# One layer of a streaming encoder: low parts of output-projection weights, two plain up-projection pairs and token sums by accumulating DMAs, and the second norm's squares and rows in more buffers

## The chip, the cores and the metric

The kernel runs on one core of a Trainium2 chip. The metric is the device time of one execution in microseconds. Before the change three runs took 1517.62, 1519.51 and 1512.99 us, a median of 1517.62.

## What is computed

A block with 16 meta tokens ahead of 1024 tokens of width 1024: a norm, then attention and a state-space model beside each other, merged by gates and projected by `w_o`; a second norm, then a gated convolutional feed-forward layer; a final norm. All in float32.

```python
def _mixer(xn, w_in, b_forget, w_attn_out, ..., w_glu, w_o):
    ...
    y_a = _forgetting_attention(q, k, v, f_logit, b_forget) @ w_attn_out
    ...
    merged = g[..., :D_MODEL] * y_a + g[..., D_MODEL:] * y_s
    return merged.astype(xn.dtype) @ w_o

def _conv_ffn(xn, w_up, conv_w, conv_b, w_down):
    hid = xn @ w_up
    hp = jnp.pad(hid, ((0, 0), (CONV_WIDTH - 1, 0), (0, 0)))
    conv = conv_b + sum(hp[:, j:j + seq_len] * conv_w[j] for j in range(CONV_WIDTH))
    val, gate = jnp.split(conv, 2, axis=-1)
    return (jax.nn.silu(gate) * val) @ w_down

def reference(x, meta_tokens, ...):
    h = jnp.concatenate([meta, x], axis=1)
    xn = _rmsnorm(h, norm_mix_g)
    h = h + _mixer(xn, ...)
    xn = _rmsnorm(h, norm_ffn_g)
    h = h + _conv_ffn(xn, w_ffn_up, ffn_conv_w, ffn_conv_b, w_ffn_down)
    return _rmsnorm(h, norm_final_g)[:, N_META:]
```

## The kernel before

**Split operands.** Every float32 matrix is kept as two tiles in a shorter matmul format: `hi`, a copy of it rounded by the copy, and `lo`, what the rounding left over. A product then takes three matmuls: hi by hi, hi by lo, lo by hi. For each operand tile somebody makes `hi` (mostly ScalarE, L940, L1113, L260; for the attention's output weights GpSimd, L149) and then `lo = source - hi`, which is `split_lo` (L128, recorded as L129) on VectorE or GpSimd. One older helper makes `lo` otherwise: `lo_by_dma` (L133) has ScalarE write minus `hi` (L135), and then a DMA issued by GpSimd adds the source from DRAM to it (L136). Before the change it serves early weights alone (`w_g`, `w_q`, `w_k`).

**Order.** The program is written as plain loops; a scheduler fixes the order of each engine's instructions when the kernel is built, and at run time each engine works through its own list in that order. DMAs stand in the list of the engine that issues them: SP (SyncE) issues the plain loads, POOL (GpSimd) the accumulating ones, and a DMA whose inputs aren't ready holds what is behind it in that list. Tiles come from pools with a set number of buffers for each tag; a tile waits until the buffer's last readers are done.

**The merge** (L948 to L963, 668.5 to 719.5 us of the span). For each of 8 row blocks `i`, `wchunk(w_ao[i], 4)` loads 128x512 weights into `raw` and makes `whi` and `wlo` (two buffers each in the pool `wp`); 36 matmuls (L958 to L960) form the attention's output, VectorE multiplies by the gate (L961) and adds into `merged[i]` (tile `mr`, L962). Beside that, `out_forms` makes the operands of products 0 and 4 of the next stage in the memory of `xhi` and `xlo`.

**The output products** (719.5 to 811.1 us). `merged` by `w_o` is done with seven products of half-size blocks (`out_product`, in the order 0, 4, 1, 5, 2, 3, 6), each with 4 blocks of tokens and 48 matmuls (L1015 to L1017). Products 1, 2, 3 and 5 use sums of weight blocks formed earlier in DRAM (`to_d`). `operands(p)` loads the weights of later products (`out_weights`, tile `wr`) and has `out_forms` make operands of the left (from `mr`) and the right (from `wr`). Of its low parts those of products 0, 4 and 5 are GpSimd's and the others VectorE's. Rows of `h2` are finished by VectorE (L1021) and, for product 2, GpSimd (L1024).

**The second norm** (`normed`, from product 6 on). For each of 9 blocks of rows: ScalarE sums the squares (L170), VectorE and GpSimd make the factor (L172, L174), VectorE scales into `xs` (L179), TensorE transposes (L187), ScalarE writes `xhi` and VectorE `xlo` (L189, L129). The squares go to the same `xs` tile, of which there are two.

**The up projection** (from 811.1 us). Pairs of gate and value columns: pair 0 and pair 1 are plain (`plain_pair`: weights in four `sw` tiles for each half, matmuls L1165 to L1167, then the convolution's taps on ScalarE L1169 and VectorE L1171, tiles `og` and `ov`). `xn_forms` makes sums of token halves for the other pairs: for each of four `k`, `fa` and `fb` by GpSimd (L1185) and VectorE (L254 to L258), then hi and lo (`t0h`, `t0l` to `t3l`). `fa` and `fb` share three buffers of the tag `h`, which later pairs use too. Pairs 2 to 20 use seven half-size products (`block_pair`, `seven`), with sums of weights by GpSimd (`sf`, L1121); the last pair, 21, is plain again. GpSimd also issues accumulating DMAs of the down projection's weight sums (L1139) from pair 2 on.

Of the kernel before, what the change touches and what calls it, by code (L numbers as in the profile page):

```python
# [9 lines left out]
F = mybir.dt.float32  # L10
# [9 lines left out]
P = 128  # L20
# [30 lines left out]
def block_kernel(ctx, tc, x, meta, g1, x0t, g1t, w_q, w_k, w_v, w_f, w_u, w_g, b_f, w_ao, lam_d, bw_d, cw_d,  # L51
# [86 lines left out]
    def wchunk(src, k, eng=None, act=False):  # L138
        raw = wp.tile([P, k, P], F, tag="raw", name="raw", padded_shape=[P, KD, P])
        ld = (GP if act else SY).dma_start(raw, src)  # L140
        if act:
            after(ld, late[0])
        hi = wp.tile([P, k, P], R, tag="whi", name="whi", padded_shape=[P, KD, P])
        lo = wp.tile([P, k, P], R, tag="wlo", name="wlo", padded_shape=[P, KD, P])
        if act:
            S.copy(hi, raw)
            lo_by_dma(lo, hi, src)
            return hi, lo
        GP.tensor_scalar(hi, raw, 1.0, 0.0, ALU.mult, ALU.add)  # L149
        split_lo(eng or V, lo, raw, hi)  # L150
        return hi, lo
# [25 lines left out]
    def norm_rows(pl, src, n, gB, xs):  # L177
        rs = norm_factor(pl, src, n, 3, xs)
        V.scalar_tensor_tensor(out=xs[:n], in0=src, scalar=rs[:n], in1=gB[:n], op0=ALU.mult, op1=ALU.mult)  # L179
# [67 lines left out]

    def token_forms(k, whole, f, T):
# [10 lines left out]
        for f_, t_ in zip((f3, f2, f1, f4), (T[2], T[1], T[0], T[3])):  # L259
            S.copy(t_[0], f_)  # L260
            split_lo(V, t_[1], f_, t_[0])
# [626 lines left out]
    merged = [mp.tile([P, LQ], F, name=f"mr{i}") for i in range(KD)]  # L888
# [30 lines left out]
    def out_weights(p, q, pl, tag, bufs=2):  # L919
# [4 lines left out]
        wr[p, 2 * q], wr[p, 2 * q + 1] = t_[:, 0], t_[:, 1]  # L924

    def out_forms(p, j):
# [12 lines left out]
        for q, src in ((0, (a11, a11, a11, a21, a12, a22, a11)[p]), (2, wr.pop((p, j)))):  # L939
            S.copy(slot[q], src)  # L940
            split_lo(GP if p in (0, 4, 5) else V, slot[q + 1], src, slot[q])
# [6 lines left out]
    for i in range(KD):  # L948
# [5 lines left out]
        whi, wlo = wchunk(w_ao[i], 4)  # L954
# [70 lines left out]

    def normed(c, dst, n):
        xs = n2.tile([P, D], F, tag="xs", name="xs", bufs=2)
        norm_rows(n2, dst, n, g2B, xs)
        to_feature(xs, n, xhi, xlo, TILES[c][0] if c else T0)
        if c:  # L1030
            SY.dma_start(h_d[P * (c - 1):P * c], dst)
# [3 lines left out]
    tags = {1: "raw", 5: "whi", 2: "wlo", 3: "raw", 6: "whi"}  # L1035
# [114 lines left out]
    def plain_pair(c, parts=(QBLK,)):  # L1150
        res = []
        ws = {}
        for part, (m, tag) in ((part, mt) for part in parts for mt in ((NFF + c, "og"), (c, "ov"))):
            if m not in ws:
                raw = up_raw(m)
                ws[m] = [split_q(raw[:, KH * q:KH * q + KH]) for q in range(2)]
# [629 lines left out]
```

## Time and profile before

| | before |
|---|---|
| runs, us | 1517.62, 1519.51, 1512.99 |
| profiled execution, its own time | 1517.67 us |
| its span, first to last instruction | 1515.9 us |
| mean granted TensorE clock | 0.983 |
| instructions | 26588 |
| merge | 668.5 to 719.5 us |
| output products | 719.5 to 811.1 us |
| end of product 6 to the start of pair 2 | 811.1 to 882.1 us |

The profile is of one execution. PE is TensorE's matmuls, PEld its weight loads, DVE VectorE, ACT ScalarE, POOL GpSimd, SP SyncE. A row of waits reads: the engine and line that waited, what ended the wait, total us, times, the longest. A row of groups reads: line, engine, operation, output from inputs, shapes, count, then busy us and the mean ns of one, then the idle time ahead of it and what ended that. In a table of windows PEclk is the TensorE clock granted, 1 being full speed, and the DMA share is that of all 16 engines. "Landing" is the time from the issue of a DMA to its end. In the page's rows L numbers are lines of the kernel before.

### The profile page before, as it was taken

Reading aid. Unit: us, or ns where it says so; the run is one execution under the profiler, and the core shown is the slowest. Engines: PE = TensorE matmul, PEld = TensorE weight load, DVE = VectorE, ACT = ScalarE, POOL = GpSimd, SP = SyncE. Lnnn points to the kernel's source line nnn. Section 1 sums busy time; section 2 is a strip of 40 time slices with the busy share of each in tenths; the row PEclk is TensorE's granted clock in tenths of the full one; section 3 lists DMA queues with packets and bytes.
Section 4 is the critical chain, followed back from the end, with each engine's and each line's share of the span. In section 5 each row is a group of like instructions: output and inputs, shape, how many; then the busy total and the mean of one; then the engine's idle time right before and its main releaser. Section 6 shows DMA issues by size and latency. Waiting matters only on the chain.

```text
span 1515.9 us, 26588 instructions
## 1 busy us (share of the span) xinstructions
PE 1447.7 (96%) x9736; PEld 1363.6 (90%) x9736; DVE 1093.1 (72%) x2178; ACT 697.6 (46%) x1351; POOL 782.2 (52%) x866
## 2 busy tenths in 40 slices
PE   7999997999999999999998799999999999999997
PEld 6989997998999999998787799999999999878886
DVE  7878748871656676645777987888887774798785
ACT  6334665531546565540435444444444444444343
POOL 1411136760546555546852645555544326599766
PEclk9999999999999999999999899999999999999999
DMA  6365572551027422164533146676643214774413
GB/s 241 94 163 141 141 139 63 164 168 51 23 78 192 128 55 92 43 251 152 211 88 135 43 105 174 174 189 180 166 114 98 73 68 167 290 238 127 138 49 111
DMA packets 88150, 201.46 MB, mean 133 GB/s; under 512 B 14330, under 2 KB 25210, under 8 KB 87636
## 3 DMA queue, kind: packets, MB, share of 16 engines
q1 hardware_dynamic: 69956, 161.83, 32.7%
q0 software_dynamic: 11840, 27.28, 10.1%
q10 hardware_dynamic: 6224, 10.65, 1.9%
q8 instruction: 77, 1.26, 0.3%
q14 instruction: 53, 0.43, 0.1%
HBM read 160.65 MB, written 69.35 MB: 152 GB/s over the span
## 4 chain that ended last, share of the span: by engine, by line
PE 78%; DVE 9%; DMA 6%; issue 3%; POOL 2%; ACT 2%; SPq 0%; POOLq 0%; DVEq 0%; ACTq 0%
PE mm L155 4%; PE mm L157 4%; PE mm L156 4%; PE sp L215 4%; PE sp L216 4%; PE sp L217 4%; PE mm L215 3%; PE tp L215 3%; PE mm L217 3%; PE tp L216 3%; PE mm L216 3%; PE tp L217 3%; PE tp L752 2%; PE po L774 1%; PE po L773 1%
## 5 line engine op out<-in xcount | busy, mean ns | idle before, releaser
L155 PE MATMUL mm<-xhi,whi 128*128 128x342 f32 (+2 forms) x488 | 159.4, 327 | 1.0 <-DVE q L129 1.0
L157 PE MATMUL mm<-xhi,wlo 128*128 128x342 f32 (+2 forms) x488 | 158.3, 325 | 0.0
L156 PE MATMUL mm<-xlo,whi 128*128 128x342 f32 (+2 forms) x488 | 157.7, 324 | 0.0
L1144 POOL TENSOR_TENSOR ov<-ov,og 128x1024 f32<-128x1024 f32 x21 | 51.3, 2441 | 130.7 <-ACT og L1143 127.9
L129 DVE TENSOR_TENSOR sw<-sf,sw 128x512 fp32r<-128x512 f32 x76 | 70.7, 931 | 52.5 <-ACT sw L1113 52.5
L1113 ACT CAST sw<-sf 128x512 fp32r<-128x512 f32 x76 | 47.5, 625 | 112.1 <-POOL sf L1121 79.2
L155 PEld LDWEIGHTS mm<-xhi,whi 128*128 128x128 f32 x488 | 91.9, 188 | 2.1 <-PE sp L710 0.8
L157 PEld LDWEIGHTS mm<-xhi,wlo 128*128 128x128 f32 x488 | 91.8, 188 | 0.3
L156 PEld LDWEIGHTS mm<-xlo,whi 128*128 128x128 f32 x488 | 91.9, 188 | 0.2
L217 PE MATMUL mm<-xhi,sw 128*128 128x256 f32 (+1 forms) x304 | 85.5, 281 | 0.0
L215 PE MATMUL mm<-xhi,sw 128*128 128x256 f32 (+1 forms) x304 | 85.3, 281 | 0.0
L216 PE MATMUL mm<-xlo,sw 128*128 128x256 f32 (+1 forms) x304 | 85.2, 280 | 0.0
L759 ACT CAST th<-tp 128x256 fp32r<-128x256 f32 (+3 forms) x120 | 56.2, 472 | 61.8 <-PE tp L752 28.1
L129 DVE TENSOR_TENSOR tl<-tp,th 128x256 fp32r<-128x256 f32 (+3 forms) x120 | 65.2, 547 | 25.8 <-ACT th L759 24.4
L724 POOL TENSOR_SCALAR pt<-pt,nm 128x144 f32<-128x144 f32 (+4 forms) x72 | 51.6, 729 | 50.7 <-DVE nm L723 49.7
L1121 POOL TENSOR_TENSOR sf<-raw,sf 128x512 f32<-128x512 f32 x38 | 62.2, 1638 | 27.4 <-DVE sw L129 27.4
L1206 DVE SCALAR_TENSOR_TENSOR ov<-hv,cwt,ov 128x1024 f32<-128x1024 f32 x38 | 74.2, 1953 | 0.2
L1121 POOL TENSOR_TENSOR sf<-raw 128x512 f32<-128x512 f32 x38 | 49.9, 1314 | 45.9 <-DVE sw L129 21.7
L1113 ACT CAST sw<-raw 128x512 fp32r<-128x512 f32 x69 | 42.4, 620 | 58.9 <-PE sp L217 27.8
L722 ACT ACTIVATE pt<-pt,nm 128x144 f32<-128x144 f32 (+4 forms) x72 | 52.9, 735 | 27.3 <-DVE nm L721 26.9
L715 DVE CUSTOM_DVE_ANT_0 pt<-sp,fb 128x328 f32<-128x328 f32 (+8 forms) x112 | 46.4, 430 | 19.5 <-PE sp L710 11.3
L129 DVE TENSOR_TENSOR sw<-raw,sw 128x512 fp32r<-128x512 f32 x69 | 57.6, 842 | 3.5 <-ACT sw L1113 2.6
(693 smaller groups left out, 5733.9 us busy)
## 6 DMA issues: line engine op xcount, KB each, us to landing
raw<-in_w_up_dram SPq DMA_DIRECT2D x44, 512.0 KB, 3.7
t_d<-in_w_dn_dram POOLq DMA_DIRECT2D x44, 256.0 KB, 6.9
ar<-a_d SPq DMA_DIRECT2D x44, 256.0 KB, 4.9
wr<-t_d SPq DMA_DIRECT2D x44, 256.0 KB, 2.9
a_d<-ov SPq DMA_DIRECT2D x21, 512.0 KB, 2.6
wr<-in_w_dn_dram SPq DMA_DIRECT2D x33, 256.0 KB, 3.4
t_d<-in_w_dn_dram SPq DMA_DIRECT2D x22, 256.0 KB, 4.7
t_d<-t_d SPq DMA_DIRECT2D x22, 256.0 KB, 4.7
```

The lines of the kernel that those rows point to most:

```text
L129: return eng.tensor_tensor(out_, src, hi.bitcast(F), ALU.subtract)
L155: yield PE.matmul(ps, whi[:, i, :], ahi[:, i], start=(i == 0), stop=False)
L156: yield PE.matmul(ps, whi[:, i, :], alo[:, i], start=False, stop=False)
L157: yield PE.matmul(ps, wlo[:, i, :], ahi[:, i], start=False, stop=(i == k - 1))
L215: PE.matmul(ps, a[0][:, i], bh, start=(i == 0 and not joins), stop=False, skip_group_check=True)
L216: PE.matmul(ps, a[0][:, i], bl, start=False, stop=False, skip_group_check=True)
L217: PE.matmul(ps, a[1][:, i], bh, start=False, stop=(i == kh - 1), skip_group_check=True)
L722: S.activation(pt[:n, :kc], pt[:n, :kc], AF.Exp, bias=nm[:n, 1:2], scale=0.125, accum_out=nm[:n, 2:3])
L759: S.copy(th[:kn, z:tw], tp[:kn, z:tw])
L1113: S.copy(hi, src)
L1121: sums.append(GP.tensor_tensor(f_, a, b, op))
L1206: V.scalar_tensor_tensor(out=o, in0=h_[:, j:SEQ + j], scalar=cwc(j, m), in1=o, op0=ALU.mult, op1=ALU.add)
```

## The change

Four edits. First, `wchunk` gets a switch `dma`, on for the eight chunks of `w_ao`: `hi` by a ScalarE copy, `lo` by `lo_by_dma`. Second, `out_forms` makes the low parts of all 28 right-hand tiles by `lo_by_dma`, from `w_o` or `to_d`; the left-hand ones stay. Third, a new `neg_lo` (VectorE writes minus `hi`, a DMA of POOL adds the source) takes the place of `split_lo` in `token_forms` (16 tiles, source the SBUF tiles `fa` and `fb`) and in `plain_pair` (12 tiles, source `w_up` in DRAM). Fourth, the second norm's squares go to a bf16 tile of their own in the `wlo` buffers of `wp`, and its rows `xs` to two buffers of `n2`, the two `whi` buffers of `wp`, the buffer of `mr0`, and, for the meta rows, in place; the `wr` tiles of product 6 move from `whi` to `wlo`. That is 8 + 28 + 16 + 12 = 64 accumulating DMAs more on POOL.

```diff
--- before.py
+++ after.py
@@ -135,14 +135,14 @@
         S.activation(lo, hi.bitcast(F), AF.Copy, scale=-1.0)
         GP.dma_start(lo, src.bitcast(R), accum_op=ALU.add)
 
-    def wchunk(src, k, eng=None, act=False):
+    def wchunk(src, k, eng=None, act=False, dma=False):
         raw = wp.tile([P, k, P], F, tag="raw", name="raw", padded_shape=[P, KD, P])
         ld = (GP if act else SY).dma_start(raw, src)
         if act:
             after(ld, late[0])
         hi = wp.tile([P, k, P], R, tag="whi", name="whi", padded_shape=[P, KD, P])
         lo = wp.tile([P, k, P], R, tag="wlo", name="wlo", padded_shape=[P, KD, P])
-        if act:
+        if act or dma:
             S.copy(hi, raw)
             lo_by_dma(lo, hi, src)
             return hi, lo
@@ -174,8 +174,8 @@
         GP.tensor_tensor(rs[:n], va[:n], nhalf[:n], ALU.pow)
         return rs
 
-    def norm_rows(pl, src, n, gB, xs):
-        rs = norm_factor(pl, src, n, 3, xs)
+    def norm_rows(pl, src, n, gB, xs, sq=None):
+        rs = norm_factor(pl, src, n, 3, sq)
         V.scalar_tensor_tensor(out=xs[:n], in0=src, scalar=rs[:n], in1=gB[:n], op0=ALU.mult, op1=ALU.mult)
 
     def to_feature(xs, n, dhi, dlo, col, bank=st_ps):
@@ -245,6 +245,10 @@
         S1, A22, S4 = split_q(s1), split_q(a22), split_q(s4)
         return [A11, S3, S2, S1, A12, A22, S4]
 
+    def neg_lo(lo, hi, src):
+        V.tensor_scalar(lo, hi.bitcast(F), -1.0, None, ALU.mult)
+        GP.dma_start(lo, src.bitcast(R), accum_op=ALU.add)
+
     def token_forms(k, whole, f, T):
 
         f1, f2, f3, f4 = f
@@ -258,7 +262,7 @@
         V.tensor_tensor(f4, f4, f2, ALU.subtract)
         for f_, t_ in zip((f3, f2, f1, f4), (T[2], T[1], T[0], T[3])):
             S.copy(t_[0], f_)
-            split_lo(V, t_[1], f_, t_[0])
+            neg_lo(t_[1], t_[0], f_)
 
     turn = [0]
 
@@ -885,7 +889,7 @@
     mm_n[1] = True
     st_o = ExitStack()
     mp = pool(st_o, "merged", side="right")
-    merged = [mp.tile([P, LQ], F, name=f"mr{i}") for i in range(KD)]
+    merged = [mp.tile([P, LQ], F, tag=f"mr{i}", name=f"mr{i}") for i in range(KD)]
 
     st_m = ExitStack()
     mg = pool(st_m, "mergein", side="left")
@@ -921,7 +925,8 @@
         t_ = pl.tile([P, 2, 512], F, tag=tag, name="wr", bufs=bufs)
         src = (o_block(*own_w[p]) if p in own_w else to_d[p])[256 * q:256 * q + 256]
         SY.dma_start(t_, src.rearrange("(c p) d -> p c d", p=P))
-        wr[p, 2 * q], wr[p, 2 * q + 1] = t_[:, 0], t_[:, 1]
+        for i in range(2):
+            wr[p, 2 * q + i] = t_[:, i], src[P * i:P * i + P]
 
     def out_forms(p, j):
 
@@ -936,9 +941,12 @@
         elif p == 6:
             GP.tensor_tensor(a11, a11, a12, sub)
         slot = slots_of[p][j]
-        for q, src in ((0, (a11, a11, a11, a21, a12, a22, a11)[p]), (2, wr.pop((p, j)))):
-            S.copy(slot[q], src)
-            split_lo(GP if p in (0, 4, 5) else V, slot[q + 1], src, slot[q])
+        a_ = (a11, a11, a11, a21, a12, a22, a11)[p]
+        S.copy(slot[0], a_)
+        split_lo(GP if p in (0, 4, 5) else V, slot[1], a_, slot[0])
+        b_, src = wr.pop((p, j))
+        S.copy(slot[2], b_)
+        lo_by_dma(slot[3], slot[2], src)
 
     ga0 = side_loads(0)
     for mm in gate_chunk(KD - 1, mg, True):
@@ -951,7 +959,7 @@
         mi = merged[i]
         if i % 2 == 0:
             out_weights((0, 4)[i // 4], i % 4 // 2, mg, "wr", 4)
-        whi, wlo = wchunk(w_ao[i], 4)
+        whi, wlo = wchunk(w_ao[i], 4, dma=True)
         for t, n in QBLK:
             ps = mm_ps()
             for m, oh, ol in os_:
@@ -1023,16 +1031,23 @@
             for d_, op in ((bot[:, l_], ALU.add), (bot[:, r_], ALU.subtract), (top[:, r_], ALU.subtract)):
                 GP.tensor_tensor(d_, d_, u2[t], op)
 
+    rows = {c: (n2, "xs", 2) for c in (5, 6, 2, 3)} | {c: (wp, "whi", 2) for c in (7, 8, 4)} | {1: (mp, "mr0", 1)}
+
     def normed(c, dst, n):
-        xs = n2.tile([P, D], F, tag="xs", name="xs", bufs=2)
-        norm_rows(n2, dst, n, g2B, xs)
+        if c:
+            pl, tag, bufs = rows[c]
+            xs = pl.tile([P, D], F, tag=tag, name="xs", bufs=bufs)
+        else:
+            xs = dst
+        sq = wp.tile([P, 2 * D], BF, tag="wlo", name="sq")
+        norm_rows(n2, dst, n, g2B, xs, sq[:, :D])
         to_feature(xs, n, xhi, xlo, TILES[c][0] if c else T0)
         if c:
             SY.dma_start(h_d[P * (c - 1):P * c], dst)
 
 
     after_of = {None: (1,), 0: (5,), 4: (2,), 5: (3, 6)}
-    tags = {1: "raw", 5: "whi", 2: "wlo", 3: "raw", 6: "whi"}
+    tags = {1: "raw", 5: "whi", 2: "wlo", 3: "raw", 6: "wlo"}
 
     def operands(p):
         for nx in after_of.get(p, ()):
@@ -1153,7 +1168,13 @@
         for part, (m, tag) in ((part, mt) for part in parts for mt in ((NFF + c, "og"), (c, "ov"))):
             if m not in ws:
                 raw = up_raw(m)
-                ws[m] = [split_q(raw[:, KH * q:KH * q + KH]) for q in range(2)]
+                ws[m] = []
+                for q in range(2):
+                    ks = slice(KH * q, KH * q + KH)
+                    hi, lo = ring()
+                    S.copy(hi, raw[:, ks])
+                    neg_lo(lo, hi, w_up[m][:, ks])
+                    ws[m].append((hi, lo))
                 res.append(conv_out(m, tag))
             w2, o = ws[m], res[len(ws) - 1 if len(ws) < 2 else int(m == c)]
             for t, n in part:
```

The edits shift later line numbers: L931 to L937 become L936 to L942, L1121 becomes L1136, L1144 L1159, L1165 to L1167 L1186 to L1188, L1171 L1192, L1185 L1206, and L254 to L258 of the token sums L258 to L262. The DMAs of `neg_lo` are L250, its negations L249.

**POOL in the merge.** The first chunks' weights, the sigmoid's last step (`gs`), the left (`mr`) and right (`wr`, `w_o`) operands of product 0. Before:

```order
L149 TENSOR_SCALAR whi<-raw 128x512
L442 TENSOR_SCALAR gs<-gs 128x1026
L129 TENSOR_TENSOR xhi<-wr,xhi 128x512 x4
L149 TENSOR_SCALAR whi<-raw 128x512
L129 TENSOR_TENSOR xhi<-mr_8508,xhi 128x512
L129 TENSOR_TENSOR xlo<-wr,xlo 128x512
L931 TENSOR_TENSOR mr_8508<-mr_8508 128x512
```

And now, in the same place:

```order
L446 TENSOR_SCALAR gs<-gs 128x1026
L136 DMA wlo<-in_w_ao_dram 128x512
L136 DMA xhi<-in_w_o_dram 128x512 x4
L136 DMA wlo<-in_w_ao_dram 128x512
L129 TENSOR_TENSOR xhi<-mr_8508,xhi 128x512
L136 DMA xlo<-in_w_o_dram 128x512
L936 TENSOR_TENSOR mr_8508<-mr_8508 128x512
```

The second chunk's high part is gone from POOL, and the transfer of its low part stands behind `gs`; the third chunk's stands behind four transfers of product 0.

**POOL behind the second norm.** The last factors of the norm, then the token sums. Before, no DMA stands there:

```order
L174 TENSOR_TENSOR rs<-vr,nhalf 128x1 x4
L1185 TENSOR_TENSOR fa<-xhi,xlo 128x514
L1185 TENSOR_TENSOR fb<-xhi,xlo 128x514
L1185 TENSOR_TENSOR fa<-xhi,xlo 128x514 x3
L1185 TENSOR_TENSOR fb<-xhi,xlo 128x514 x2
L1185 TENSOR_TENSOR fa<-xhi,xlo 128x514 x2
```

And now:

```order
L174 TENSOR_TENSOR rs<-vr,nhalf 128x1 x4
L1206 TENSOR_TENSOR fa<-xhi,xlo 128x514
L1206 TENSOR_TENSOR fb<-xhi,xlo 128x514
L1206 TENSOR_TENSOR fa<-xhi,xlo 128x514 x3
L250 DMA sw<-in_w_up_dram 128x512 x5
L1206 TENSOR_TENSOR fb<-xhi,xlo 128x514
L250 DMA sw<-in_w_up_dram 128x512
L250 DMA t2l<-fb 128x514
L250 DMA sw<-in_w_up_dram 128x512 x2
L250 DMA t0l<-fa 128x514
```

The low parts of pair 0's weights (`sw`) come behind five token sums, and the later token sums behind those transfers.

**TensorE at the end of the second norm.** The last transposes (L187) and pair 0. Before, matmuls of pair 0 stand between them:

```order
L187 MATMUL sp<-ident,xs 128x128 x4
L187 MATMUL tp<-ident,xs 128x128 x4
L1167 MATMUL po<-xhi,sw 128x256
L1165 MATMUL po<-xhi,sw 128x256
L1166 MATMUL po<-xlo,sw 128x256
L1167 MATMUL po<-xhi,sw 128x256
```

And now:

```order
L187 MATMUL sp<-ident,xs 128x128 x4
L187 MATMUL tp<-ident,xs 128x128 x4
L1186 MATMUL mm<-xhi,sw 128x258
L1187 MATMUL mm<-xlo,sw 128x258
L1186 MATMUL mm<-xhi,sw 128x256
L1187 MATMUL mm<-xlo,sw 128x256
```

All transposes of the norm now come first, and pair 0 begins with the matmuls by its weights' high part.

## The prediction, made before the change was run

> **What bounds the kernel now.** First the page's busy line and its chain of work by engine.
>
> ```profile
> span 1515.9 us, 26588 instructions
> PE 1447.7 (96%) x9736; PEld 1363.6 (90%) x9736; DVE 1093.1 (72%) x2178; ACT 697.6 (46%) x1351; POOL 782.2 (52%) x866
> PE 78%; DVE 9%; DMA 6%; issue 3%; POOL 2%; ACT 2%; SPq 0%; POOLq 0%; DVEq 0%; ACTq 0%
> ```
>
> TensorE works 96% of the span. No matmul is removed, so only its gaps, and time at a low clock, can change. All 64 new transfers lie where the table by stage puts the merge (first row), the output products (second), and the norm with pairs 0 and 1 (third); the fourth is the first ordinary pair, the fifth and sixth lie around one stall.
>
> ```profile
> core 0: us, PE busy (x) PEld busy (x) DVE busy (x) ACT busy (x) POOL busy (x), PEclk, DMA share, GB/s
> 668.50:719.50 51.00, 47.41 (x290) 46.69 (x289) 28.59 (x38) 10.22 (x17) 36.87 (x36) 0.97 0.63 221
> 719.50:811.10 91.60, 88.83 (x398) 71.31 (x397) 71.02 (x81) 38.02 (x69) 58.38 (x48) 0.98 0.49 174
> 811.10:882.10 71.00, 57.26 (x385) 56.11 (x384) 62.59 (x85) 33.88 (x62) 35.73 (x27) 0.86 0.16 45
> 882.10:902.10 20.00, 20.00 (x171) 20.00 (x169) 15.52 (x24) 7.95 (x15) 11.30 (x8) 1.00 0.42 123
> 685.00:690.00 5.00, 1.57 (x10) 1.28 (x9) 1.64 (x4) 0.00 (x0) 5.00 (x6) 0.94 0.21 82
> 690.00:695.00 5.00, 5.00 (x24) 4.85 (x25) 4.15 (x4) 0.62 (x1) 3.11 (x4) 0.72 0.37 95
> ```
>
> TensorE's waits between 655 and 900 us, by what ended them:
>
> ```profile
> PE mm L1165 <- DVE og L1171: 11.2, 2, 8.5
> PE mm L958 <- POOL whi L149: 3.4, 1, 3.4
> PE sp L1015 <- DVE h L1021: 2.8, 1, 2.8
> PE sp L187 <- DVE xs L179: 2.6, 1, 2.6
> ```
>
> The merge loses 3.4 us to POOL and (1 - 0.72) x 5 = 1.4 us of clock behind it; the products lose 2.8. The third stage loses most. A matmul of 256 to 258 columns takes 20.00/171 = 0.117 us at full clock. Pair 0 has 192 of these, 22.5 us; pair 1 has 144 of 342 to 344 columns, and at 0.117 x 343/257 = 0.156 us they need 22.5; the 48 transposes need about 5. That is 50 of 71 us: **21 us** are lost there, 13.7 idle and the rest at low clock. The chain between 811 and 885 us says to whom:
>
> ```profile
> by line: issue 9.1%; PE mm L1165 9.1%; PE mm L1166 8.7%; PE mm L1167 8.1%; DVE fa L255 6.0%; DVE sw L129 5.7%; DVE fa L257 5.4%; DVE t2l L129 5.3%; DVE t1l L129 3.9%; PE sp L187 3.7%; DVE og L1171 3.7%; DVE fb L254 3.2%; ACT xhi L189 2.9%;
> 833.98 4.98 issue
> 870.46 1.46 DVE og L1171 x3
> ```
>
> VectorE's sums and subtractions (L254 to L258, L129) hold the `og` steps that free pair 1's banks.
>
> **Part A: the eight w_ao chunks.** Rows of POOL, VectorE and ScalarE; the older accumulating transfers (L136, with their times to landing), and queue 0 from 900 to 1100 us:
>
> ```profile
> 668.79 0.62 POOL L149 TENSOR_SCALAR whi<-raw 128x512 fp32r<-128x512 f32 x1 [13.06 <-PE po L156]
> 669.94 1.68 POOL L442 TENSOR_SCALAR gs<-gs 128x1026 f32<-128x1026 f32 x1 [0.53 <-ACT gs L436]
> 672.49 6.26 POOL L129 TENSOR_TENSOR xhi<-wr,xhi 128x512 fp32r<-128x512 f32 x4 [0.87 <-ACT xhi L940]
> L129 DVE TENSOR_TENSOR wlo<-raw,whi 128x512 fp32r<-128x512 f32 x7 | 7.6, 1088 | 5.2 <-POOL whi L149 5.1
> L940 ACT CAST xhi<-mr 128x512 fp32r<-128x512 f32 x12 | 7.4, 620 | 23.9 <-DVE mr L962 17.0 <-PE tp L1016 6.7
> L136 POOL DMA_DIRECT2D wlo<-in_w_g_dram x7: 862/872/1222, 73.1 to 171.4; - x7
> DMA to landing us min/median/max: 6.3/7.3/13.1
> q0 software_dynamic: 5184, 9.44, 29.1%
> L1139 POOL DMA_DIRECT2D t_d<-in_w_dn_dram x44: 796/1122/1758, 873.8 to 1158.7; - x44
> DMA to landing us min/median/max: 3.7/5.7/8.9
> t_d<-in_w_dn_dram POOLq DMA_DIRECT2D x44, 256.0 KB, 6.9
> ```
>
> Removed: eight POOL copies of 0.62 us, eight VectorE subtractions of 1.09, the 3.4 us wait and its 1.4 of clock: **-5**. Added for a chunk: two ScalarE passes (0.62 each, the negation taken like the cast) and one POOL issue of 0.87. An accumulating 512 KB lands after 6.3 to 13.1 us. Queue 0 moved 9.44 MB in 29.1% of 200 us, 58.2 us; 36 pieces of 256 KB, **1.6 us** each. One 256 KB lands between 3.7 and 8.9 (L1139's landing row, which mixes POOL and SP issues; POOL's own have a median of 6.9 where they queue behind one another). A 512 KB piece less 1.6 us of traffic is 4.7 at its least and 5.7 at its median; I take **5** for a piece with none ahead.
>
> The second chunk's transfer stands on POOL behind L442, whose end is 671.6; issued at 672.5 it lands at 677.5, and the first chunk's matmuls end about 674.5. Some of the next chunk's `whi` matmuls are pulled ahead, so I count 2 to 3 us. The third stands behind the four `xhi` transfers, which share the queue with loads: four pieces at 1.6 put it 4.5 us late. The fourth costs about 3. Later chunks turn two buffers round in 0.62 + 0.62 + 5 = 6.2 us where a chunk's 36 matmuls take 36 x 0.156 = 5.6 and some have been waited for: at most 1 us a chunk, and clock of about 2. Costs together +8, so A is **+3**. If transfers land in 3.7 all waits but one go (-4); at 8.9 each of the first three waits grows by 2 (+9).
>
> **Part B: 28 right-hand tiles.** Of these 12 came from POOL and 16 from VectorE:
>
> ```profile
> L129 POOL TENSOR_TENSOR xhi<-wr,xhi 128x512 fp32r<-128x512 f32 x8 | 11.7, 1496 | 3.1 <-PE tp L995 2.2 <-ACT xhi L940 0.9
> L129 DVE TENSOR_TENSOR op<-wr,op 128x512 fp32r<-128x512 f32 x8 | 7.5, 934 | 0.0
> L129 DVE TENSOR_TENSOR xlo<-wr,xlo 128x512 fp32r<-128x512 f32 x4 | 6.9, 1772 | 0.0
> 755.00:760.00 5.00, 3.15 (x9) 2.55 (x10) 4.19 (x6) 1.14 (x2) 1.91 (x2) 0.77 0.08 21
> ```
>
> POOL gives up 1.50 us a tile and gets 0.87; VectorE gives up 0.93 to 1.77 a tile; ScalarE gets 28 x 0.62 = 17.4 us beside the 38 of 91.6 that it is busy. Most of this lies beside matmuls. What can return is the 2.8 us wait at L1015 and 1.7 of clock around 752 to 765. New waits: the last tile of product 5 stands behind ScalarE's and POOL's work for product 2, and by the same steps lands about 1 us after it is wanted. B is **-3**; nothing gained and two late tiles would be +2, the whole and a smoother product 6 -5.
>
> **Part C: norm, pair 0, token sums, pair 1.** Rows of the norm's steps, the token sums and their low parts:
>
> ```profile
> L170 ACT ACTIVATE xs<-h 128x1024 f32<-128x1024 f32 x8 | 8.5, 1067 | 7.1 <-DVE h L1021 7.1
> L179 DVE SCALAR_TENSOR_TENSOR xs<-h,rs,g2B 128x1024 f32<-128x1024 f32 x8 | 11.3, 1410 | 2.4 <-POOL rs L174 2.3
> L1185 POOL TENSOR_TENSOR fb<-xhi,xlo 128x514 f32<-128x514 f32 x8 | 12.2, 1521 | 7.2 <-DVE fa L255 4.4 <-DVE t1l L129 2.8
> L129 DVE TENSOR_TENSOR t1l<-fa,t1h 128x514 fp32r<-128x514 f32 x4 | 4.9, 1224 | 0.0
> L172 DVE TENSOR_SCALAR vr<-ss 128x1 f32<-128x1 f32 (+1 forms) x9 | 1.3, 147 | 3.4 <-ACT xs L170 3.3
> 832.17 0.69 DVE L129 TENSOR_TENSOR xlo<-tp,xhi 128x512 fp32r<-128x512 f32 x1 [0.16 <-ACT xhi L189]
> 830.00:835.00 5.00, 2.33 (x12) 1.96 (x11) 3.55 (x9) 3.00 (x6) 2.91 (x3) 0.50 0.00 0
> ```
>
> Call E the end of product 6 (811.1). The norm's last `xlo` ended at 832.9, E + 21.8. Its own work on VectorE for five rows is 5 x (0.15 + 1.41 + 1.4) = 15, part of it before E; without the wait for two shared buffers, and without pair 0's `og` steps between, I take **E + 10**. Gain at the norm: 11. But pair 0's first low parts now need this row: POOL does five token sums ahead of the first `sw` transfer (5 x 1.3 = 6.4, at the speed that L1185 has with VectorE quiet, below its mean 1.52), then issue and landing. First low tile: E + 10 + 6.4 + 5 = **E + 21**. Before, pair 0's matmuls ran from E on beside the transposes. From there 45 us of pairs 0 and 1 and 2.5 of clock (as the 0.50 of the last row takes 2.5 in 5 us): E + 68.5.
>
> Then pair 2 needs all token forms. A VectorE negation of this size is in no row. Its cost lies between the 0.15 of L172 and the 1.22 of `t1l`; I take the 0.69 of a subtraction that reads PSUM, since the source is one SBUF tensor. It spares some 0.5 x 28 = 14 us of VectorE. A token group now ends at its landing, and its three shared buffers (`h`) come free only then. Eight `sw` and four token transfers at 1.6 end group 0 at E + 16.4 + 19 = E + 36; three further groups at about 12 each (four L1185, some 6 us, and a landing of 6, the sums of the next group beside it) end at **E + 72**. Pair 2 waits 3.5 us: it starts at E + 72 to 73, and started at 882.1 = E + 71. C is **+2**. With sums at once and landings of 3.7 it is E + 62 (-9); with groups that don't overlap +14 or more (below).
>
> The last plain pair has its weights long before; its four transfers run under pair 20's 20 us of matmuls and cost nothing; late, they would cost one landing, 5 us.
>
> **Sum:** +3 - 3 + 2 = **+2**. The profiled execution took 1517.67, 0.05 above the median 1517.62, and 1.8 beyond its span: **1520 us**.
>
> A rule of the Trainium skill weighed here, "DMA: Bandwidth & Descriptors", section "Anatomy of one DMA — SWDGE (gpsimd) path": such a transfer takes about 2.0 us and its bytes at 436 GB/s. For 512 KB that is 3.2, where the rows have 6.3 to 13.1, so the trace disagrees for the accumulating kind; by it A would be -5 and C about -5, and the time 1505.
>
> **Rivals.**
>
> *Faster:* transfers land at the 3.7 us of the best row. Then a merge buffer turns in 4.9 us, under 5.6, and A is -5; B is -4; token groups come before E + 68 and C is -5. Sum -14, **1504**. For it: the norm stage's DMA share is 0.16. Against: the median row, 5.7. Chance 0.24; the rule above speaks for this case.
>
> *Slower, by in-order waits for `h`:* POOL holds every token group until the last one has landed, and all behind it. A group then costs 6 (sums) + 2.8 (two VectorE sums) + 0.6 + 0.7 + 0.9 + 6.9 = 18: the last ends at E + 36 + 54 = E + 90 in place of 72, **1537**. It decides when a group takes over 11 us (E + 36 + 3 x 11), since pair 1 ends at E + 68.5. For it: one queue, three buffers. Against: a third buffer lets one sum go ahead. Chance 0.20.
>
> *Slower, by the VectorE negation:* POOL's issue has been seen to take 1758 ns, twice its 872, when VectorE is busy. 24 issues at +0.9 are 21 us of POOL, about two thirds on the token chain: +14, **1534**. Against: L136's issues with VectorE busy keep to 862 to 1222. Chance 0.08. The Trainium skill, "SBUF — State Buffer", section "Who interferes with whom", says that a VectorE `tensor_scalar` can take both port pairs and keep GpSimd from writing descriptors; no row here shows it.
>
> *The change doesn't shorten the norm:* its chain (1.07, 0.15, 0.66 on POOL, 1.41, transposes, copies) may bind and not the buffers. The norm then ends at E + 21 and everything in C moves by 11: **1531**. Chance 0.06.
>
> **How the numbers follow.** Forecast 0.42, within 0.5% (7.6 us, about what a measurement of this kernel can tell from no change). Faster 0.24. Slower 0.20 + 0.08 + 0.06 = 0.34. The range takes in the faster rival and the dearest slower one, 1503 to 1537; that leaves out about 0.2.
>
> **What would show it.** Right: no L149 wait in the merge but TensorE waiting on `wlo` landings up to 4 us; the last transpose near E + 10; the first low-part matmul of pair 0 near E + 21; pair 2 waiting on a token landing. Wrong: pair 0's first low part before E + 15, merge waits under 2 us in sum, or a POOL line of L1185 waits that runs past pair 1 by over 8 us.

## Result and profile after

Four runs of the changed kernel took 1535.32, 1535.88, 1541.58 and 1536.84 us, a median of 1536.36; before, 1517.82 (four runs, 1512.99 to 1519.51). The ratio is **1.0134, with a 95% interval of 1.0102 to 1.0167**: slower by 1.3%. Forecast was no change, 1520 us.

The page of the changed kernel: busy line, queues, and the chain by engine.

```profile
span 1533.5 us, 26738 instructions
PE 1451.1 (95%) x9736; PEld 1364.7 (89%) x9736; DVE 1061.1 (69%) x2154; ACT 720.6 (47%) x1395; POOL 805.8 (53%) x910
...
q1 hardware_dynamic: 69956, 161.83, 32.0%
q0 software_dynamic: 21056, 44.08, 16.6%
...
PE 73%; DMA 10%; DVE 8%; POOL 3%; ACT 3%; issue 2%; SPq 1%; POOLq 0%; DVEq 0%; ACTq 0%
```

VectorE lost 32 us of work, as the change means it to. On the chain TensorE's share fell from 78% to 73%, and DMA's rose from 6% to 10%. The table by stage: merge, output products, the end of product 6 to the first matmul of pair 2, and pair 2. Then TensorE's waits between 655 and 930 us.

```profile
663.70:729.30 65.60, 51.00 (x290) 48.76 (x289) 22.50 (x31) 21.79 (x39) 31.84 (x37) 0.90 0.83 231
729.30:816.10 86.80, 86.80 (x396) 69.92 (x395) 44.59 (x63) 46.86 (x89) 61.53 (x64) 1.00 0.72 190
816.10:892.10 76.00, 57.16 (x385) 54.56 (x384) 57.19 (x80) 32.38 (x58) 49.62 (x43) 0.89 0.67 159
892.10:920.20 28.10, 22.39 (x173) 22.21 (x172) 21.63 (x32) 10.03 (x18) 18.80 (x16) 0.88 0.72 163
```

```profile
PE mm L1188 <- DMA sw<-in_w_up_dram: 9.4, 1, 9.4
PE mm L968 <- DMA wlo<-in_w_ao_dram: 8.7, 3, 6.7
PE mm L215 <- ACT ov L1190: 5.7, 1, 5.7
PE mm L1186 <- DVE og L1192: 5.4, 2, 3.9
PE sp L187 <- DVE xlo L129: 2.4, 3, 1.1
PE po L968 <- DMA wlo<-in_w_ao_dram: 2.6, 2, 1.4
```

The waits on POOL's `whi` and on `h` are gone; waits on landings of accumulating transfers stand first. With E for the end of product 6 (810.2 before, 816.1 after; the forecast's 811.1 lies 0.9 us behind it, among the transposes), stage by stage. Part C is counted to the start of the 169th matmul of L215 to L217 behind E, since a pair has 168 of them and some kernels pull the first matmuls of a pair ahead:

| stage, us | before | after | difference | forecast |
|---|---|---|---|---|
| merge (A) | 51.0 | 65.6 | +14.6 | +3 |
| output products (B) | 90.5 | 86.8 | -3.7 | -3 |
| E to the start of pair 3 (C) | 91.8 | 103.7 | +11.9 | +2 |

The forecast's +2 is for the start of pair 2: its first matmul came at E + 71.8 before and comes at E + 76.0 now, and pair 2 then takes longer. The stages sum to +22.8. The spans differ by 17.6 and the medians by 18.5. The profiled execution of before took long ahead of the merge, 668.7 us, where that of after took 663.7 and the twelve profiles below 662.5 to 668.1; and in the later rounds before had medians of 1514.2 to 1515.1, below the 1517.8 here. So runs are compared by stage, and whole times by their ratios.

### The profile page after: what moved, and what is told of

The parts are those of the page before. It is cut to its first block, busy times and chain, and to the rows that moved or that the text cites. A ratio compares the mean times of both kernels' runs of the same rounds, so it can differ in the third digit from the quotient of the medians.

```text
span 1533.5 us, 26738 instructions
## 1 busy us (share of the span) xinstructions
PE 1451.1 (95%) x9736; PEld 1364.7 (89%) x9736; DVE 1061.1 (69%) x2154; ACT 720.6 (47%) x1395; POOL 805.8 (53%) x910
## 4 chain that ended last, share of the span: by engine, by line
PE 73%; DMA 10%; DVE 8%; POOL 3%; ACT 3%; issue 2%; SPq 1%; POOLq 0%; DVEq 0%; ACTq 0%
PE sp L215 4%; PE sp L216 4%; PE sp L217 4%; PE mm L157 4%; PE mm L155 4%; PE mm L156 4%; PE mm L215 3%; PE mm L217 3%; PE mm L216 3%; PE tp L215 3%; PE tp L216 3%; PE tp L217 3%; PE tp L756 2%; PE po L778 2%; PE po L777 2%
## 5 line engine op out<-in xcount | busy, mean ns | idle before, releaser
L129 DVE TENSOR_TENSOR sw<-sf,sw 128x512 fp32r<-128x512 f32 x76 | 74.8, 984 | 54.2 <-ACT sw L1128 54.1
L1159 POOL TENSOR_TENSOR ov<-ov,og 128x1024 f32<-128x1024 f32 x21 | 51.0, 2427 | 115.2 <-ACT og L1158 114.1
L1128 ACT CAST sw<-sf 128x512 fp32r<-128x512 f32 x76 | 47.4, 624 | 110.6 <-POOL sf L1136 80.3
L157 PEld LDWEIGHTS mm<-xhi,wlo 128*128 128x128 f32 x488 | 91.8, 188 | 0.3
L215 PE MATMUL mm<-xhi,sw 128*128 128x256 f32 (+1 forms) x304 | 86.0, 283 | 5.7 <-ACT ov L1190 5.7
L217 PE MATMUL mm<-xhi,sw 128*128 128x256 f32 (+1 forms) x304 | 86.0, 283 | 0.0
L1136 POOL TENSOR_TENSOR sf<-raw 128x512 f32<-128x512 f32 x38 | 51.7, 1361 | 43.7 <-DVE sw L129 22.3
L1136 POOL TENSOR_TENSOR sf<-raw,sf 128x512 f32<-128x512 f32 x38 | 62.5, 1644 | 22.6 <-DVE sw L129 22.6
L726 ACT ACTIVATE pt<-pt,nm 128x144 f32<-128x144 f32 (+4 forms) x72 | 52.9, 735 | 25.9 <-DVE nm L725 25.3
L215 PEld LDWEIGHTS mm<-xhi,sw 128*128 128x128 f32 x304 | 57.8, 190 | 5.9 <-ACT ov L1190 5.9
L719 DVE CUSTOM_DVE_ANT_0 pt<-sp,fb 128x328 f32<-128x328 f32 (+8 forms) x112 | 46.4, 430 | 20.3 <-PE sp L714 12.1
L756 PE MATMUL tp<-ident,pt 128*128 128x128 f32 (+1 forms) x360 | 58.2, 270 | 0.1
```

The costliest lines, as they stand in the source:

```text
L129: return eng.tensor_tensor(out_, src, hi.bitcast(F), ALU.subtract)
L157: yield PE.matmul(ps, wlo[:, i, :], ahi[:, i], start=False, stop=(i == k - 1))
L215: PE.matmul(ps, a[0][:, i], bh, start=(i == 0 and not joins), stop=False, skip_group_check=True)
L217: PE.matmul(ps, a[1][:, i], bh, start=False, stop=(i == kh - 1), skip_group_check=True)
L726: S.activation(pt[:n, :kc], pt[:n, :kc], AF.Exp, bias=nm[:n, 1:2], scale=0.125, accum_out=nm[:n, 2:3])
L756: PE.transpose(tp[:kn, o:o + n], p_[:n, k0:k0 + kn], ident[:n, :n])
```

## Where the merge's time went

Three rows of the changed kernel's timeline in the merge (start, duration, engine, line; in brackets the idle time before and what ended it), and the DMA queues of 660 to 690 us (packets, MB, share of 16 engines):

```profile
672.59 0.90 POOL L136 DMA_DIRECT2D wlo<-in_w_ao_dram  x1
685.78 0.65 PE L968 MATMUL mm<-k,wlo 128*128 128x342 f32 x1 [6.74 <-DMA wlo<-in_w_ao_dram]
689.42 0.62 ACT L146 CAST whi<-raw 128x512 fp32r<-128x512 f32 x1 [4.75 <-DMA raw<-in_w_ao_dram]
```

```profile
DMA  9999999999999999999999999999999999999999
...
q1 hardware_dynamic: 2642, 7.25, 64.7%
q0 software_dynamic: 1220, 2.24, 40.4%
...
raw<-in_w_ao_dram SPq DMA_DIRECT2D x2, 256.0 KB, 19.7
```

The third chunk's transfer was issued at 672.6, 8.9 us into the merge, and landed 13 us later, not 5. The 16 DMA engines are, on average, at least 90% busy in every slice. The accumulating queue moved 2.24 MB in 12.1 us of all engines (0.404 x 30), 5.4 us per MB; the plain queue 7.25 MB in 19.4, 2.7 per MB. An accumulated byte takes **twice** the engine time of a loaded one. The queue is not the reason: in the kernel before, between 55 and 65 us, POOL's queue carries three plain loads and nothing else, 1.57 MB in 41.4% of 10 us, 2.6 us per MB:

```profile
q0 software_dynamic: 432, 1.57, 41.4%
```

The two queues share the engines: the plain `raw` of the fourth chunk came late as well, in 19.7 us.

Two theories were tried apart: traffic, or the chunks' own chain of cast, negation, issue and landing with two buffers. The first three kernels start from the changed one. The whole times in what was expected of them were reckoned from 1517.8 us; before ran at 1515.1 in their round.

Undo all 16 transfers of the merge (`e1_no_merge`):

```diff
-        whi, wlo = wchunk(w_ao[i], 4, dma=True)
+        whi, wlo = wchunk(w_ao[i], 4)
...
-        lo_by_dma(slot[3], slot[2], src)
+        if p in (0, 4):
+            split_lo(GP, slot[3], b_, slot[2])
+        else:
+            lo_by_dma(slot[3], slot[2], src)
```

> Undoes in the changed kernel the accumulating transfers of the merge: the eight w_ao chunks and the right-hand operands of products 0 and 4 are made by subtraction again. Theory (the merge is bound by DMA traffic, which these 16 transfers lengthen): the merge takes 51 us again where the changed kernel has 65.6, the products keep 87, and the whole is 14 us shorter than the changed kernel, about 1522. Rival (the merge is longer because it starts 5 us earlier, ahead of loads that arrive when they did): merge 56, whole 1527.

Measured: merge 51.1, products 86.8, whole 1520.49, ratio 1.0039 (1.0021 to 1.0057). Its merge began at 665.8, and that of `e4_best1` below, which took 51.1 us as well, at 662.5, ahead of the changed kernel's 663.7. So the earlier start is not the cause. What is left above before is C.

Undo the eight chunks only, the first two lines above (`e2_no_ao`):

> Undoes only the eight w_ao chunks (high part by POOL, low part by subtraction); the eight operands of products 0 and 4 stay accumulating. Theory (traffic: 8 pieces at 1.5 us of all DMA engines while these are full, which holds up the plain loads as well): the merge stays above the 51 us of before, at 56 to 60, whole about 1528. Rival (what costs is the chunks' own chain of cast, negation, issue and landing behind other work on POOL): merge 51 to 52, whole about 1522.

Measured: merge **55.7**, whole 1522.72, ratio 1.0058 (1.0037 to 1.0079). The merge is just under the theory's 56 to 60 and well above the rival's 51 to 52; the whole is the rival's. The row behind it, of this kernel's POOL, shows a plain load held up. It took 16.7 us to land (at most 5.3 before), and TensorE's wait for `whi` grew from 3.4 to 6.3 us.

```profile
685.67 0.61 POOL L149 TENSOR_SCALAR whi<-raw 128x512 fp32r<-128x512 f32 x1 [2.48 <-DMA raw<-in_w_ao_dram]
```

Undo the operands of products 0 and 4 only, the last lines above (`e3_no_of04`):

> Undoes only the right-hand operands of products 0 and 4; the eight w_ao chunks stay accumulating. Theory (traffic): three pieces, 4.5 us, remain in the time in which the DMA engines are full; the chunk's transfer lands in 5 to 7 us in place of 13; merge 54 to 57, whole about 1527. Rival (the chunks' own chain with two buffers): merge 62 or more, whole 1533 or more.

Measured: merge **55.7**, inside the theory's 54 to 57; whole 1530.81, ratio 1.0094 (1.0069 to 1.0118), above the theory's 1527; its C is 104.4. TensorE's waits for `wlo` were 7.3 in sum, and the longest 2.2:

```profile
PE mm L971 <- DMA wlo<-in_w_ao_dram: 3.7, 3, 2.1
PE po L971 <- DMA wlo<-in_w_ao_dram: 3.6, 2, 2.2
```

Either eight pieces cost 4.7 us, both together 14.6. A cost that grows faster than the number of pieces fits full engines; a chain of fixed landings would not give it. The landings say the same: 13 us for the third chunk's transfer, 19.7 and, in `e2_no_ao`, 16.7 for a plain load.

## Where the time behind product 6 went

In the changed kernel the norm's last `xlo` ends at 826.5, E + 10.4, and TensorE's first low part of pair 0 comes at E + 21.1. Both are as forecast, and so far nothing is lost. Then these rows, in order of time, of TensorE, POOL, VectorE and ScalarE, and two rows of groups, the last token tile (`t3l`) in the changed kernel and in the one before (shortest, median and longest in ns, then first and last start):

```profile
837.25 0.58 PE L1188 MATMUL mm<-xhi,sw 128*128 128x258 f32 x1 [9.45 <-DMA sw<-in_w_up_dram]
855.76 1.79 POOL L1206 TENSOR_TENSOR fb<-xhi,xlo 128x514 f32<-128x514 f32 x1 [6.64 <-DMA t1l<-fa]
873.03 3.56 POOL L1206 TENSOR_TENSOR fa<-xhi,xlo 128x514 f32<-128x514 f32 x2 [2.20 <-DMA t3l<-fb]
889.31 0.69 DVE L258 TENSOR_TENSOR fb<-fa 128x514 f32<-128x514 f32 x1 [3.32 <-DMA t1l<-fa]
889.39 1.77 POOL L1206 TENSOR_TENSOR fb<-xhi,xlo 128x514 f32<-128x514 f32 x1 [2.23 <-DMA t1l<-fa]
897.91 0.62 ACT L264 CAST t1h<-fa 128x514 fp32r<-128x514 f32 x1 [2.35 <-DVE fa L261]
898.96 0.63 ACT L1190 ACTIVATE ov<-mm,cwt 128x340 f32<-128x340 f32 x1
899.66 0.55 PE L215 MATMUL mm<-xhi,sw 128*128 128x256 f32 x1 [5.71 <-ACT ov L1190]
L250 POOL DMA_DIRECT2D t3l<-fb x4: 862/866/873, 846.9 to 905.4; - x4
L129 DVE TENSOR_TENSOR t3l<-fb,t3h x4: 680/780/1382, 846.1 to 886.6; 128x514 fp32r<-128x514 f32 x4
```

A buffer of `h` is free when the transfers that read it have landed. A group takes two of the three buffers, so POOL can sum the next group's `fa` ahead, but `fb`, which POOL and VectorE (L258) both write, must wait for a landing: POOL's `fb` of the second group at 855.8, the last group's `fa` at 873.0 and its `fb` at 889.4, 11.1 us in the three. The last transfers of the four groups are issued between 846.9 and 905.4, so a group takes (905.4 - 846.9) / 3 = 19.5 us. Before, with subtractions and no landing, it took (886.6 - 846.1) / 3 = 13.5. The forecast had 12. TensorE doesn't wait on the last landing, which is what the forecast expected, but on what stands behind the token work on in-order engines: ScalarE's `ov` stands behind `t1h` of the last group, and pair 2's bank behind `ov`.

From here the stretch is C, E to the start of pair 3.

| kernel | stretch, us |
|---|---|
| before | 91.8 |
| changed; the eight chunks undone, products 0 and 4 undone, both undone (e2, e3, e1) | 103.7, 102.0, 104.4, 101.8 |
| e4: no merge transfers, no negations | 93.2 |
| e5: token sums undone | 96.3 |
| e6: plain pairs undone | 97.4 |
| e7: negations on ScalarE | 99.5 |

Take out the merge's transfers and all of `neg_lo` (`e4_best1`): the edits of `e1_no_merge`, and

```diff
-            neg_lo(t_[1], t_[0], f_)
+            split_lo(V, t_[1], f_, t_[0])
...
-                    neg_lo(lo, hi, w_up[m][:, ks])
+                    split_lo(V, lo, raw[:, ks], hi)
```

> Keeps of the change only the accumulating operands of products 1, 2, 3, 5 and 6 and the norm's buffers; merge, token sums and plain pairs are as before. Theory (these two parts gain what the others lose): the products take 87 in place of 90.5 us, the norm's last low part comes 10 to 12 us after product 6 in place of 22, and the stretch up to pair 3 is 3 to 8 us shorter than before: whole 1507 to 1512. Rival (VectorE's token sums bind that stretch whatever the norm does): products -3.5 alone, whole 1513 to 1515.

Measured: products 86.8, stretch 93.2, whole 1513.23, ratio 0.9982 (0.9970 to 0.9994). The norm ends 12 us earlier (E + 10.4, 22.7 before) and nothing comes of it; the rival's numbers came. Two rows of the table by windows of this kernel, from E + 20 and E + 30 on, and TensorE's longest wait in the stretch:

```profile
820.50:830.50 10.00, 6.50 (x54) 6.32 (x54) 10.00 (x13) 3.61 (x8) 5.96 (x4) 1.00 0.46 157
830.50:840.50 10.00, 10.00 (x85) 10.00 (x84) 10.00 (x16) 4.64 (x9) 6.40 (x4) 1.00 0.01 2
PE mm L1189 <- DVE og L1195: 11.0, 3, 6.7
```

VectorE (DVE busy, 10.00 of 10.00) has no idle time there. TensorE has 3.5 us in the first row, and in the stretch it waits longest for VectorE's `og`.

Undo the token sums alone, the first of these two edits (`e5_no_tok`):

> Undoes in the changed kernel only the token sums' low parts (VectorE subtracts again); plain pairs, merge and the rest as changed. From the end of product 6 to the start of pair 3 before has 92 us and the changed kernel 104. Theory (each token group holds its shared buffers until its transfers have landed, 16 to 17 us a group): without these 16 transfers the stretch is 92 to 96 us, whole about 1526. Rival (the negations on VectorE and POOL's sums and issues block each other, and pair 0 waits for its weights' transfers): eight negations and transfers of pairs 0 and 1 remain, the stretch is 98 to 101 us, whole about 1532.

Measured: stretch 96.3, whole 1531.68, ratio 1.0106 (1.0080 to 1.0132). Just past the theory's end and short of the rival's 98; the whole is longer than expected.

Undo the plain pairs alone, the second (`e6_no_pp`):

> Undoes only the plain pairs' low parts (VectorE subtracts again); the token sums keep negation and transfer. Theory (held buffers): pair 0 starts 12 us after product 6 in place of 21, but the token groups still take 14 us or more each, and the stretch from product 6 to pair 3 is 98 to 102 us, whole about 1532. Rival (what costs is pair 0's wait of 9.4 us for its first weights): the stretch is 93 to 95, whole about 1526.

Measured: stretch 97.4, whole 1533.58, ratio 1.0127 (1.0107 to 1.0148), nearer to the theory's 98 than to the rival's 95. Above e4's 93.2, the pairs' transfers alone (e5) cost 3.1 us and the tokens' alone (e6) 4.2; together 10.5 in the changed kernel and 8.6 in e1, which has e4's merge. They share one queue, and together cost more than their sum. POOL's group waits remain in e6, but shorter, and a group takes 18.0 us by the last transfers; in e5, with the token transfers alone gone, it takes 12.1 by the last subtractions, and in e4 12.7. So the landings make a token group some 6 us longer. First e6, then e5:

```profile
POOL fb L1206 <- DMA t1l<-fa: 4.5, 2, 3.6
L250 POOL DMA_DIRECT2D t3l<-fb x4: 862/877/1287, 848.3 to 902.2; - x4
```

```profile
L129 DVE TENSOR_TENSOR t3l<-fb,t3h x4: 679/1220/1781, 848.8 to 885.2; 128x514 fp32r<-128x514 f32 x4
```

Put the 28 negations on ScalarE (`e7_act_neg`):

```diff
-        V.tensor_scalar(lo, hi.bitcast(F), -1.0, None, ALU.mult)
+        S.activation(lo, hi.bitcast(F), AF.Copy, scale=-1.0)
```

> The changed kernel with all 28 negations of the plain pairs and the token sums on ScalarE in place of VectorE; transfers as changed. Theory (held buffers and landings): token groups still 14 us or more each; the stretch from product 6 to pair 3 is 100 to 104 us, whole 1532 to 1536. Rival (VectorE's negation and POOL block each other: up to 3.1 us an issue, 1.3 a negation, where 0.87 and 0.41 were seen without it): issues go back to 0.87, the first low part of pair 0 lands 4 to 6 us earlier, the stretch is 92 to 97 us, whole 1524 to 1529.

Measured: stretch 99.5 (in a profiled execution of 1530.05 us, the least of the four), whole 1535.84, ratio 1.0141 (1.0111 to 1.0170). The stretch lies between the two; the rival's mark, a first low part 4 to 6 us earlier, did not come (E + 22.1, where the changed kernel has 21.1). Its issues and POOL's waits:

```profile
L250 POOL DMA_DIRECT2D sw<-in_w_up_dram x12: 852/1350/3601, 830.7 to 1265.1; - x12
```

```profile
POOL fb L1206 <- DMA t1l<-fa: 11.0, 3, 6.0
```

Issues of over 3 us come without any negation on VectorE, so it is not what makes them long; the group waits are there in full. In the changed kernel a negation did suffer while POOL summed, these two rows of VectorE:

```profile
826.44 5.36 DVE L249 TENSOR_SCALAR sw<-sw 128x512 fp32r<-128x512 f32 x4
833.40 0.41 DVE L249 TENSOR_SCALAR sw<-sw 128x512 fp32r<-128x512 f32 x1
```

1.34 us each against 0.41. The Trainium skill, "SBUF — State Buffer", section "Who interferes with whom", says that a `tensor_scalar` can take the port pair that VectorE shares with GpSimd, and that the one of the two that comes later is then blocked; the first row agrees with that for VectorE's side. By e7, with the negations off VectorE, at most 4.2 of the stretch's 11.9 us hang on it, and the whole was no shorter.

## Which parts are worth keeping

Pairs 1 and 21 by ScalarE's negation and transfer, on top of e4 (`e8_best2`):

```diff
-                    split_lo(V, lo, raw[:, ks], hi)
+                    if c == 0:
+                        split_lo(V, lo, raw[:, ks], hi)
+                    else:
+                        lo_by_dma(lo, hi, w_up[m][:, ks])
```

> As the kernel that keeps only products 1, 2, 3, 5, 6 and the norm's buffers (1513.2), and besides that pairs 1 and 21 (not pair 0) by ScalarE's negation and accumulating transfer. Theory (after the shorter norm VectorE is full, 10.0 of every 10 us, and sets that stretch): four subtractions less there, 3 to 5 us: the stretch from product 6 to pair 3 is 88 to 90 us where that kernel has 93, whole about 1509. Rival (pair 1 waits for its low parts' landing behind the token sums on POOL): the stretch is 93 or more, whole 1513 or more.

Measured: stretch 95.2, whole 1514.11, ratio 1.0003 (0.9990 to 1.0016). The number is the rival's, but not its mechanism: no wait of TensorE there ends with a landing, and the longest are again for VectorE's `og`, 11.3 us in three. VectorE stays full: a token sum (L258) beside POOL's work took 3.95 us there, where e4's longest took 1.80. Four subtractions less gave nothing.

The last token group alone, on top of e4 (`e11_last_group`):

```diff
-            split_lo(V, t_[1], f_, t_[0])
+            if k == KH - 1:
+                lo_by_dma(t_[1], t_[0], f_)
+            else:
+                split_lo(V, t_[1], f_, t_[0])
```

> As the kernel that keeps only products 1, 2, 3, 5, 6 and the norm's buffers (stretch 93.2 us), and the last of the four token groups alone by ScalarE's negation and accumulating transfer; no later token sum waits for its buffers. Theory (a token transfer costs by the buffer it holds; VectorE is full): four subtractions less on VectorE, 2 to 4 us: the stretch is 89 to 92 us, whole about 1511. Rival (any landing on the way to pair 2 costs, held buffer or not): the last low parts land 5 to 9 us later than a subtraction, the stretch is 95 us or more, whole 1515 or more.

Measured: stretch 92.2, whole 1511.76, ratio 0.9977 (0.9963 to 0.9991); 1.0 us below e4's stretch, near the upper end of what was expected, and no landing is paid. The interval overlaps with e4's, so a gain isn't shown; a transfer whose buffers nobody waits for was about free.

Products 1, 2, 3, 5 and 6 alone, put into the kernel before (`e9_of_only`; the lines that make the right-hand operands):

```diff
...
+        S.copy(slot[2], b_)
+        if p in (0, 4):
+            split_lo(GP, slot[3], b_, slot[2])
+        else:
+            lo_by_dma(slot[3], slot[2], src)
```

> The kernel before with one part of the change alone: the right-hand operands of products 1, 2, 3, 5 and 6 by accumulating transfers; merge, norm, token sums and pairs as before. Theory (the 3.7 us that the products lost came from this part, and the norm's new buffers give nothing by the start of pair 3): products 86 to 87 us, from there to pair 3 90 to 92 as before, whole 1510.5 to 1512 beside 1514.6. Rival (the products are shorter because of the norm's buffers, whose first rows run beside product 6): products 90, whole 1514 to 1515.

Measured: products 86.1, stretch 90.7, whole **1508.22, ratio 0.9955 (0.9939 to 0.9970)**: faster than both kernels. Its transfers run where the DMA engines had room (share 0.49 in the products before, 0.86 now), and TensorE is busy in all of the 86.1 us.

The norm's buffers alone; all low parts by subtraction (`e10_norm_only`):

```diff
-        whi, wlo = wchunk(w_ao[i], 4, dma=True)
+        whi, wlo = wchunk(w_ao[i], 4)
...
-        lo_by_dma(slot[3], slot[2], src)
+        split_lo(GP if p in (0, 4, 5) else V, slot[3], b_, slot[2])
...
-            neg_lo(t_[1], t_[0], f_)
+            split_lo(V, t_[1], f_, t_[0])
...
-                    neg_lo(lo, hi, w_up[m][:, ks])
+                    split_lo(V, lo, raw[:, ks], hi)
```

> The norm's buffers alone; every low part is made by subtraction as before. Theory (VectorE is full behind the norm): the norm's last low part comes about 10 us after product 6 in place of 22, the products keep 90 us, and the stretch from product 6 to pair 3 stays within 91 to 94 us: whole 1514 to 1516. Rival (the shorter norm pays where no transfer disturbs the products): the stretch is 85 us or less, whole 1508 or less.

Measured: products 89.8, stretch 95.4, whole 1517.52, ratio 1.0012 (1.0000 to 1.0023). The shorter norm pays nothing, and the stretch is 3.6 us longer than before.

A cause for that suggested itself: buffers in `wp` keep memory that pair 0's weights use next, so that eight subtractions that before ran at 780 to 793 us fall behind the norm. To try it, only the squares were put into `wp`; the rows stay in two buffers (`e12_held_memory`, from e4, with the `xs` of rows 1 to 8 in `n2`):

```diff
-    rows = {c: (n2, "xs", 2) for c in (5, 6, 2, 3)} | {c: (wp, "whi", 2) for c in (7, 8, 4)} | {1: (mp, "mr0", 1)}
+    rows = {c: (n2, "xs", 2) for c in range(1, 9)}
```

> As the kernel with products 1, 2, 3, 5 and 6 alone (1508.2, stretch from product 6 to pair 3 of 91.1 us), but the norm's squares go to a tile of the weight pool, as in the change; its rows stay in the two buffers of before. The tile keeps the pool's memory, which the up weights' buffers use next, until the norm ends. Theory (what the norm's edit takes is the early load and splitting of pair 0's weights, whose eight subtractions then fall into the time in which VectorE is full): the loads are issued after the norm's last rows, the stretch is 95 us or more, whole 1512 or more. Rival (the norm's edit costs by its order of rows or by contention): the stretch stays at 89 to 92 us, whole 1506 to 1509.

Measured: stretch 89.2, whole 1508.23, ratio 0.9945 (0.9925 to 0.9966), with e9 the fastest; their intervals overlap. The loads were held, to 807 us, and still nothing was lost: this theory **fell**. Four of pair 0's subtractions, first in e4, which differs by this one edit, and then in e12:

```profile
810.81 6.46 DVE L129 TENSOR_TENSOR sw<-raw,sw 128x512 fp32r<-128x512 f32 x4
```

```profile
819.58 2.49 DVE L129 TENSOR_TENSOR sw<-raw,sw 128x512 fp32r<-128x512 f32 x4
```

In e12 pair 0 runs between the norm's rows, as before, POOL's token sums begin at 827 us, and the subtractions take 0.62 us each. In e4, as in e10, all transposes come first; the subtractions meet POOL's first token sums (810.4 to 818.4 us) and take 1.62. Four of them make 4.0 us on a full VectorE, and the two stretches differ by 4.0 (93.2 and 89.2). No kernel changed this alone, so it stays an argument.

## Why the forecast was wrong

**What binds**: right in kind. Both losses begin with landings that TensorE, or an engine ahead of it, waits for; the last plain pair cost nothing (25.9 us, 27.4 before). Of its own signs, TensorE's wait for `wlo` came, but longer (6.7 us, up to 4 expected), and pair 2's wait for a token landing did not.

**Part A is the step that failed most**: the landing that it priced at 5 us. The forecast said that a piece "with none ahead" lands in 5 us, and that four pieces at 1.6 us put the third chunk 4.5 us late. The wait was where it said, but 13 us passed from issue to landing. The 1.6 us a piece were about right (5.4 us per MB make 1.4 for 256 KB). What it left out are the loads: it counted the pieces of POOL's queue alone, and of the merge's DMA shares it showed the stage's mean, 0.63, and two windows behind the waits, 0.21 and 0.37. At the place of the waits the engines were already full before the change, 0.99, which it did not show or price. The window of before, and one of the changed kernel (columns as in the tables by stage, the last but one the DMA share):

```profile
660.00:685.00 25.00, 24.84 (x158) 24.56 (x157) 10.89 (x12) 9.09 (x15) 14.73 (x11) 1.00 0.99 379
```

```profile
695.00:700.00 5.00, 3.19 (x12) 2.91 (x12) 1.50 (x2) 0.62 (x1) 2.48 (x3) 0.55 0.91 238
```

Before, the share was down to 0.21 at 685 to 690 us, 16 us into the merge; now it is still 0.91 at 695 to 700, 31 us into it, and plain loads are late too. A measured +14.6, past its own upper bound of +9: TensorE's idle time in the merge grew by 11.0 us (14.6, 3.6 before), and its busy time by 3.6 (51.0, 47.4 before), at a granted clock of 0.90 in place of 0.97. The upper bound was also summed too low: a landing of 8.9 us is 3.9 above the 5, not 2, and three such waits would have made A about +15. e1 to e3 show that the 16 transfers cost this; that it is by traffic rests on the full engines and the late landings.

**Part B** was right: -3 forecast, -3.7 measured, -4.4 alone (e9). The wait at L1015 and the low clock that it named are gone: TensorE is busy in all of the 86.8 us, at a clock of 1.00.

**Part C**: the norm's end (E + 10) and pair 0's first low part (E + 21) came out to the microsecond. The token group was mis-sized: 12 us forecast, 19.5 measured, and 13.5 before even without a landing. The 12 are four sums and a landing; VectorE's sums, the cast, the negation and the issue between them, 5.0 us in the forecast's own rival (with two of VectorE's four sums), were left out, since the next group's sums were to run beside the landing. Only `fa` could; `fb` waited for a buffer. That is the rival "in-order waits for `h`", with its 18 us. That rival's time, 1537, is near the measured 1536.4, but in part by chance: it put all of the loss into C, about +19 where +11.9 was measured, with A at +3. That the measured time lies within the stated range is due to that rival's price, and so to the same chance. What TensorE then waited for was a bank behind ScalarE's in-order list. A negation, taken as 0.69 us, took 0.41 undisturbed and over 1 us beside POOL's sums, so VectorE was spared less there than forecast.

**The rivals.** Faster: refuted, landings were not near 3.7 us. First the transfers in the merge, then those behind product 6:

```profile
DMA to landing us min/median/max: 4.7/7.7/13.2
DMA to landing us min/median/max: 3.3/6.2/12.9
```

The negation's blocking: by e7 at most 4.2 of C's 11.9 us, and not what makes POOL's issues long. A norm that doesn't shorten: refuted, it did; but the 11 us that the forecast counted for it gained nothing in e4 and e10, where VectorE is full behind it. That VectorE binds there rests on its full rows and on TensorE's waits for it; e8 and e11, which took four operations off it, gained 1.0 us at most.

## What to carry to other kernels

Before a low part is moved to an accumulating DMA, look at the DMA share of the very microseconds in which it will run, not of the stage, and count an accumulated byte as two, as it was here. Such a transfer cost nothing where the engines had room and nobody waited for its buffers (products 1, 2, 3, 5, 6). It holds its source until it lands, so a short ring of source buffers adds the landing to the period of the loop. A shorter stage bought nothing here where an engine of the next one was already full.

## What the runs showed of the hardware

An accumulating DMA took 5.4 us of all 16 engines per MB against 2.7 for a plain one in the same 30 us; plain loads by the accumulating queue took 2.6 (before, 55 to 65 us). A VectorE negation of a 128x512 tile took 0.41 us where a subtraction took 0.62 (e12); beside POOL's sums they took 1.34 (the changed kernel) and 1.62 (e4). POOL's DMA issues, 0.86 to 0.90 us for the merge's `wlo`, took up to 3.4 behind the norm, and up to 3.7 with no negation on VectorE (e7); what lengthens them isn't shown.
